# Feed-forward products of a decoder layer: 320 + 320 activation columns against the high weights, recut into two stretches of other widths

## The chip, the cores and the metric

The kernel runs on one NeuronCore of a Trainium2 chip. The metric is the device time of one execution in microseconds (us). Before the change it is 2118.0 us, the median of two runs (2117.37 and 2118.63). A measurement of this kernel tells a difference of about 2% from no change.

## What is computed

One decoder layer over 256 prompt tokens and 64 sample tokens, which the kernel carries side by side as 320 columns. The change touches its last part, the feed-forward block:

```python
hf = _rmsnorm(x, p['norm_ffn'])
x = x + (jax.nn.silu(hf @ p['w_ffn_gate']) * (hf @ p['w_ffn_up'])) @ p['w_ffn_down']
```

The width of `x` is 2048, the hidden width 5632, everything is float32. The rest (input projection, state-space branch, linear attention, memory attention, merge, output projection) is not touched.

## The kernel before, in words

Everything is stored transposed: features on the 128 partitions, the 320 tokens along the free dimension. A matrix product is done one block of 128 output features at a time. `load` brings the block's weights (1 MB, `raw`, three buffers) from memory, `parts` splits them into a high part `whi` (rounded to float32r, ScalarE, L79) and a low part `wlo = raw - whi` (VectorE, L80), two buffers each. The activations are split in the same way, here into `fh`/`fl` (input of the block) and `hidh`/`hidl` (hidden values). `mm3` (L91 to L93) sums three float32r products per 128 input features in one PSUM bank: high x high, high x low, low x high. Each of these matmuls is 128 x 128 weights by 320 columns and brings its own load of the weights.

The feed-forward block, `back`, runs in four quarters (`FQ`) of 11 hidden blocks (`FT`). Per hidden block there are a gate product and an up product, each over 16 chunks of 128 inputs (48 matmuls); their epilogues (L1202 to L1208 and `split`, L1073 and L1074) make one chunk of the hidden values. Then come 16 down products over the quarter's 11 hidden chunks (33 matmuls each), which are added to `x` (L1214). That makes 44 + 44 + 64 = 152 products with 12 x 176 = 2112 groups of three matmuls. In the last quarter `stats` sums squares for the final norm, whose `rstd` and scaling close the kernel. PSUM tiles come from `psum_mm`, which alternates between two pools (`pmm`, `psm`).

The order of the instructions on each engine is set by a scheduler when the kernel is built (`schedule_with_timeline_sim=True`). Engines run their instructions in that order and wait for each other through semaphores.

Of the kernel before, what the change touches and what calls it, by code (L numbers as in the profile page):

```python
# [8 lines left out]
F32 = mybir.dt.float32  # L9
F32R = mybir.dt.float32r  # L10
# [3 lines left out]
ALU = mybir.AluOpType  # L14
# [4 lines left out]
P = 128  # L19
D = 2048  # L20
KD = D // P
NP_, NS = 256, 64
NT = NP_ + NS
# [13 lines left out]
FT = FH // P // FQ  # L37
# [12 lines left out]
class Build:  # L50
# [36 lines left out]
    def mm3(self, ps, hi, lo, k0, nk, xh, xl, kx=0):  # L87
        nc = self.nc
        for k in range(nk):
            ws = slice((k0 + k) * P, (k0 + k + 1) * P)  # L90
            nc.tensor.matmul(ps, hi[:, ws], xh[:, kx + k, :], start=k == 0, stop=False)  # L91
            nc.tensor.matmul(ps, hi[:, ws], xl[:, kx + k, :], start=False, stop=False)  # L92
            nc.tensor.matmul(ps, lo[:, ws], xh[:, kx + k, :], start=False, stop=k == nk - 1)  # L93

    def together(self, products):

        first = products[0]().ins
        with self.tc.issue_after(first):
            for p in products[1:]:
                p()  # L100
# [975 lines left out]
    def back(self):  # L1076
        nc, io = self.nc, self.io
        TT = nc.vector.tensor_tensor
# [6 lines left out]
        for n, d in (("x", self.d_yx), ("g", self.d_yg)):  # L1085
            hi = yp.tile([P, 8, NT], F32R, name=f"y{n}h")
            lo = yp.tile([P, 8, NT], F32R, name=f"y{n}l")
# [15 lines left out]
        hi = yp.tile([P, 8, NT], F32R, name="ysh")  # L1103
        lo = yp.tile([P, 8, NT], F32R, name="ysl")
# [9 lines left out]
        for m2 in range(4):  # L1114
            wh, wl = self.unit(io["w_glu"][m2])
            for i in range(2):
                m = 2 * m2 + i
                ps = self.psum_mm()
# [38 lines left out]
        fp = self.push(self.left, "ffn", bufs=1)  # L1157
        x = fp.tile([P, KD, NT], F32, name="x")
        for c in range(4):
            nc.sync.dma_start(x[:, 4 * c : 4 * c + 4, :], io["xT"][:, 4 * c : 4 * c + 4, :])  # L1160
        fh = fp.tile([P, KD, NT], F32R, name="fh")
        fl = fp.tile([P, KD, NT], F32R, name="fl")
        ssum = fp.tile([P, NTP], F32, name="ssum")
        slast = fp.tile([P, NTP], F32, name="slast")
        for z in (ssum, slast):
# [3 lines left out]
        def stats(m):  # L1169
            sq = {0: ssum, KD - 1: slast}.get(m)  # L1170
            if sq is None:
                sq = fp.tile([P, NT], F32, name="sq", tag="sq", bufs=2)
            nc.scalar.square(sq[:, :NT], x[:, m, :])
            if m == KD - 1:
                return [ssum, slast]
            if m:
                TT(ssum[:, :NT], ssum[:, :NT], sq[:], op=ALU.add)

        for m in range(KD):
            wh, wl = self.unit(io["w_out"][m])  # L1180
            ps = self.psum_mm()
# [8 lines left out]
        nc.scalar.copy(rstd[:], self.rstd(sums, NT, 1.0 / D))  # L1190
        self.pop(self.right)
        dp = self.push(self.right, "hid", bufs=1)
        hh = dp.tile([P, FT, NT], F32R, name="hidh")
        hl = dp.tile([P, FT, NT], F32R, name="hidl")
        for q in range(FQ):
            for i in range(FT):
                m = q * FT + i
                wh, wl = self.unit(io["w_fg"][m])
                pg = self.psum_mm()
                self.mm3(pg[:, :NT], wh, wl, 0, KD, fh, fl)  # L1200
                s = dp.tile([P, NT], F32, name="fs", tag="fs", bufs=2)
                TT(s[:], pg[:, :NT], rstd[:], op=ALU.mult)  # L1202
                nc.scalar.activation(s[:], s[:], AF.Silu)
                TT(s[:], s[:], rstd[:], op=ALU.mult)
                wh, wl = self.unit(io["w_fu"][m])
                pu = self.psum_mm()
                self.mm3(pu[:, :NT], wh, wl, 0, KD, fh, fl)
                TT(s[:], pu[:, :NT], s[:], op=ALU.mult)  # L1208
                self.split(hh[:, i, :], hl[:, i, :], s[:])
            for m in range(KD):  # L1210
                wh, wl = self.unit(io["w_fd"][q, m], FT * P)
                ps = self.psum_mm()
                self.mm3(ps[:, :NT], wh, wl, 0, FT, hh, hl)
                TT(x[:, m, :], x[:, m, :], ps[:, :NT], op=ALU.add)  # L1214
                if q == FQ - 1:
                    sums = stats(m)
                    nc.scalar.mul(x[:, m, :], x[:, m, :], self.vec[:, C_FIN + m : C_FIN + m + 1])
# [120 lines left out]
```

## Time and profile before

| | |
|---|---|
| runs | 2117.37, 2118.63 us |
| profiled execution | 2118.14 us, of which the span of its instructions 2116.4 us |
| TensorE (PE) busy | 2088.3 us (99%), 14404 matmuls |
| VectorE (DVE) / ScalarE (ACT) busy | 1294.6 us (61%) / 848.8 us (40%) |
| DMA | 362.23 MB, mean 171 GB/s |

Times in the rows are in us from the first instruction, durations of single instructions in ns where a view says so. Matmuls overlap: a row of 0.31 us is a matmul from its start to its last result, while the next one starts earlier. So the cost of one in a stream is the distance between two starts. PE is the matmul stream, PEld the weight loads beside it.

### The profile page before, as it was taken

How to read it: one execution, taken by the hardware profiler on the slowest of the kernel's cores; microseconds unless marked ns; L12 is line 12 of the kernel's file. 1: busy time of each engine (PE TensorE's matmuls, PEld its weight loads, DVE VectorE, ACT ScalarE, POOL GpSimd, SP SyncE). 2: the span in 40 equal slices, each digit the busy share in tenths (PEclk: the TensorE clock that was granted, in tenths of full speed). 3: DMA queues.
4: the chain of work that ended last, by engine and by line, in shares of the span. 5: the costliest groups of instructions: out<-in, count | busy, mean ns of one | idle time of the engine just before them, and what ended most of it. 6: DMA issues, size and time to landing. Idle time of an engine off the chain costs nothing.

```text
span 2116.4 us, 34013 instructions
## 1 busy us (share of the span) xinstructions
PE 2088.3 (99%) x14404; PEld 2039.8 (96%) x14404; DVE 1294.6 (61%) x1964; ACT 848.8 (40%) x1117; POOL 161.3 (8%) x203
## 2 busy tenths in 40 slices
PE   9899999999999999999999999999999999999997
PEld 7899998999999999999999999999999999999997
DVE  7868779888997945675645444444444444444444
ACT  6445345554445344543434333233322333233343
POOL 8611011012101000000000000000000000000000
PEclk9999999999999999999999999999999999999998
DMA  9665665435454454765554443454434443454442
GB/s 342 216 221 207 216 215 182 149 132 184 140 178 149 149 191 156 263 208 192 199 182 152 140 158 125 148 167 159 140 129 170 160 140 129 151 179 142 145 137 105
DMA packets 72697, 362.23 MB, mean 171 GB/s; under 512 B 8032, under 2 KB 18144, under 8 KB 42720
## 3 DMA queue, kind: packets, MB, share of 16 engines
q1 hardware_dynamic: 72544, 360.05, 49.8%
q8 instruction: 113, 1.85, 0.4%
q14 instruction: 40, 0.33, 0.0%
HBM read 338.49 MB, written 21.53 MB: 170 GB/s over the span
## 4 chain that ended last, share of the span: by engine, by line
PE 91%; DVE 6%; ACT 1%; issue 1%; DMA 1%; SPq 0%; DVEq 0%; ACTq 0%
PE pmm L93 19%; PE pmm L91 19%; PE pmm L92 18%; PE psm L91 10%; PE psm L92 10%; PE psm L93 10%; DVE wlo L80 1%; DVE xr L355 0%; DVE s_w L626 0%; PE psm L903 0%; ACT whi L79 0%; PE psm L306 0%; PE psm L754 0%; PE bu L607 0%; PE psm L307 0%
## 5 line engine op out<-in xcount | busy, mean ns | idle before, releaser
L79 ACT CAST whi<-raw 128x2048 fp32r<-128x2048 f32 (+3 forms) x308 | 538.9, 1751 | 952.2 <-issue 536.8
L80 DVE TENSOR_TENSOR wlo<-raw,whi 128x2048 fp32r<-128x2048 f32 (+3 forms) x308 | 647.9, 2104 | 279.1 <-ACT whi L79 277.3
L93 PE MATMUL pmm<-hh,wlo 128*128 128x320 f32 x1408 | 438.6, 312 | 2.6 <-DVE wlo L80 2.6
L91 PE MATMUL pmm<-hh,whi 128*128 128x320 f32 x1408 | 439.2, 312 | 0.0
L92 PE MATMUL pmm<-hl,whi 128*128 128x320 f32 x1408 | 437.7, 311 | 0.0
L93 PEld LDWEIGHTS pmm<-hh,wlo 128*128 128x128 f32 x1408 | 264.4, 188 | 6.5 <-DVE wlo L80 3.1
L91 PEld LDWEIGHTS pmm<-hh,whi 128*128 128x128 f32 x1408 | 264.5, 188 | 5.8 <-issue 5.5
L92 PEld LDWEIGHTS pmm<-hl,whi 128*128 128x128 f32 x1408 | 264.5, 188 | 2.0 <-issue 1.3
L91 PE MATMUL psm<-fh,whi 128*128 128x320 f32 x704 | 217.6, 309 | 0.0
L91 PE MATMUL pmm<-fh,whi 128*128 128x320 f32 x704 | 217.6, 309 | 0.0
L92 PE MATMUL pmm<-fl,whi 128*128 128x320 f32 x704 | 217.6, 309 | 0.0
L92 PE MATMUL psm<-fl,whi 128*128 128x320 f32 x704 | 217.5, 309 | 0.0
L93 PE MATMUL psm<-fh,wlo 128*128 128x320 f32 x704 | 217.5, 309 | 0.0
L93 PE MATMUL pmm<-fh,wlo 128*128 128x320 f32 x704 | 217.5, 309 | 0.0
L91 PEld LDWEIGHTS psm<-fh,whi 128*128 128x128 f32 x704 | 132.1, 188 | 0.1
L92 PEld LDWEIGHTS pmm<-fl,whi 128*128 128x128 f32 x704 | 132.1, 188 | 0.0
L93 PEld LDWEIGHTS pmm<-fh,wlo 128*128 128x128 f32 x704 | 132.1, 188 | 0.0
L91 PEld LDWEIGHTS pmm<-fh,whi 128*128 128x128 f32 x704 | 132.1, 188 | 0.0
L92 PEld LDWEIGHTS psm<-fl,whi 128*128 128x128 f32 x704 | 132.1, 188 | 0.0
L93 PEld LDWEIGHTS psm<-fh,wlo 128*128 128x128 f32 x704 | 132.1, 188 | 0.0
L93 PE MATMUL pmm<-hidh,wlo 128*128 128x320 f32 x352 | 109.2, 310 | 0.0
L92 PE MATMUL pmm<-hidl,whi 128*128 128x320 f32 x352 | 108.8, 309 | 0.0
(431 smaller groups left out, 3687.1 us busy)
## 6 DMA issues: line engine op xcount, KB each, us to landing
raw<-w_in SPq DMA_DIRECT2D x88, 1024.0 KB, 4.9
raw<-w_fg SPq DMA_DIRECT2D x44, 1024.0 KB, 4.8
raw<-w_fu SPq DMA_DIRECT2D x44, 1024.0 KB, 4.9
raw<-w_fd SPq DMA_DIRECT2D x64, 704.0 KB, 4.1
raw<-w_br SPq DMA_DIRECT2D x24, 1024.0 KB, 4.9
at_kv<-kv SPq DMA_DIRECT2D x32, 512.0 KB, 6.3
raw<-w_out SPq DMA_DIRECT2D x16, 1024.0 KB, 4.9
raw<-w_mk SPq DMA_DIRECT2D x8, 1024.0 KB, 6.2
```

What stands on the lines that cost most here:

```text
L79: nc.scalar.copy(hi[:, s], raw[:, s])
L80: nc.vector.tensor_tensor(lo[:, s], raw[:, s], hi[:, s].bitcast(F32), op=ALU.subtract)
L91: nc.tensor.matmul(ps, hi[:, ws], xh[:, kx + k, :], start=k == 0, stop=False)
L92: nc.tensor.matmul(ps, hi[:, ws], xl[:, kx + k, :], start=False, stop=False)
L93: nc.tensor.matmul(ps, lo[:, ws], xh[:, kx + k, :], start=False, stop=k == nk - 1)
```

## The change

A new function `mm2` takes the place of `mm3` in the three products of the feed-forward block, and nowhere else. The high and the low part of the activations now lie side by side in one tile of 640 columns per chunk (`fx`, `hid`). The high weights meet these 640 columns in two matmuls of `cut` and `640 - cut` columns, which go to two PSUM banks `pa` and `pb`. The low weights meet the first 320 columns as before. So the three results are no longer summed in one bank: ScalarE copies the first 320 columns of `pa` into a tile `fsum`, and VectorE adds the rest of `pa` (if `cut` is over 320) and `pb` to it. `cut` differs by quarter and product:

| quarter | gate | up | down |
|---|---|---|---|
| 1 | 384 + 256 | 320 + 320 | 512 + 128 |
| 2 | 352 + 288 | 448 + 192 | 416 + 224 |
| 3 | 336 + 304 | 400 + 240 | 480 + 160 |
| 4 | 384 + 256 | 384 + 256 | 384 + 256 |

PSUM pairs now come in a cycle of three (`bu`, `pmm`, `psm`).

```diff
+    def mm2(self, hi, lo, nk, x, cut):
+        nc = self.nc
+        self.turn += 1
+        if self.turn % 3 == 0:
+            bu = self.pbu.tile([P, 2, 512], F32, name="bu", tag="bu", bufs=1)
+            pa, pb = bu[:, 0], bu[:, 1]
+        elif self.turn % 3 == 1:
+            pa, pb = (self.pmm.tile([P, 512], F32, name="pmm", tag="pmm", bufs=2)[:] for _ in range(2))
+        else:
+            pa, pb = (self.psum_sm()[:] for _ in range(2))
+        for k in range(nk):
+            ws = slice(k * P, (k + 1) * P)
+            nc.tensor.matmul(pa[:, :cut], hi[:, ws], x[:, k, :cut], start=k == 0, stop=False)
+            nc.tensor.matmul(pb[:, : 2 * NT - cut], hi[:, ws], x[:, k, cut:], start=k == 0, stop=k == nk - 1)
+            nc.tensor.matmul(pa[:, :NT], lo[:, ws], x[:, k, :NT], start=False, stop=k == nk - 1)
+        s = self.sums.tile([P, NT], F32, name="fsum", tag="fsum", bufs=2)
+        n = cut - NT
+        TT = nc.vector.tensor_tensor
+        nc.scalar.copy(s[:], pa[:, :NT])
+        if n:
+            TT(s[:, :n], s[:, :n], pa[:, NT:cut], op=ALU.add)
+        TT(s[:, n:], s[:, n:], pb[:, : 2 * NT - cut], op=ALU.add)
+        return s
...
-        fh = fp.tile([P, KD, NT], F32R, name="fh")
-        fl = fp.tile([P, KD, NT], F32R, name="fl")
+        fx = fp.tile([P, KD, 2 * NT], F32R, name="fx")
+        fh, fl = fx[:, :, :NT], fx[:, :, NT:]
...
-        hh = dp.tile([P, FT, NT], F32R, name="hidh")
-        hl = dp.tile([P, FT, NT], F32R, name="hidl")
+        hx = dp.tile([P, FT, 2 * NT], F32R, name="hid")
+        hh, hl = hx[:, :, :NT], hx[:, :, NT:]
+        self.sums = dp
+        cuts = ((384, 320, 512), (352, 448, 416), (336, 400, 480), (384, 384, 384))
...
-                pg = self.psum_mm()
-                self.mm3(pg[:, :NT], wh, wl, 0, KD, fh, fl)
+                pg = self.mm2(wh, wl, KD, fx, cuts[q][0])
...
-                pu = self.psum_mm()
-                self.mm3(pu[:, :NT], wh, wl, 0, KD, fh, fl)
+                pu = self.mm2(wh, wl, KD, fx, cuts[q][1])
...
-                ps = self.psum_mm()
-                self.mm3(ps[:, :NT], wh, wl, 0, FT, hh, hl)
+                ps = self.mm2(wh, wl, FT, hx, cuts[q][2])
```

Up to the first feed-forward product the order of the instructions is the same on every engine. In the block it differs at two kinds of places.

On VectorE, in the first quarter, one gate and one up epilogue with the weight splits between them stood so before:

```order
L1202 TENSOR_TENSOR fs_12548<-pmm_12499,rstd_11252 128x320
L80 TENSOR_TENSOR wlo_12613<-raw_12610,whi_12612 128x2048
L1204 TENSOR_TENSOR fs_12548<-fs_12548,rstd_11252 128x320
L1208 TENSOR_TENSOR fs_12548<-psm_12558,fs_12548 128x320
L80 TENSOR_TENSOR wlo_12672<-raw_12669,whi_12671 128x2048
L1074 TENSOR_TENSOR hidl_12258<-fs_12548,hidh_12257 128x320
```

Now the same stretch (`bu_12389` is the gate product, `pmm_12453` the up product) reads:

```order
L80 TENSOR_TENSOR wlo_12511<-raw_12508,whi_12510 128x2048
L117 TENSOR_TENSOR fsum_12438<-fsum_12438,bu_12389 128x64
L118 TENSOR_TENSOR fsum_12438<-fsum_12438,bu_12389 128x256
L1229 TENSOR_TENSOR fs_12442<-fsum_12438,rstd_11251 128x320
L1231 TENSOR_TENSOR fs_12442<-fs_12442,rstd_11251 128x320
L80 TENSOR_TENSOR wlo_12575<-raw_12572,whi_12574 128x2048
L118 TENSOR_TENSOR fsum_12502<-fsum_12502,pmm_12453 128x320
L1234 TENSOR_TENSOR fs_12442<-fsum_12502,fs_12442 128x320
L1100 TENSOR_TENSOR hid_12256<-fs_12442,hid_12256 128x320
```

The sums stand behind the weight split that becomes possible at the same product end, not ahead of it.

On TensorE, where the second quarter goes over from the up to the down products (`pmm_15495` is the first down product, `psm_15536` the second), the order before had, around the last chunk of the first one:

```order
L93 MATMUL pmm_15495<-hidh_12257,wlo_15492 128x320
L91 MATMUL psm_15536<-hidh_12257,whi_15532 128x320
L92 MATMUL psm_15536<-hidl_12258,whi_15532 128x320
L91 MATMUL pmm_15495<-hidh_12257,whi_15491 128x320
L93 MATMUL psm_15536<-hidh_12257,wlo_15533 128x320
L91 MATMUL psm_15536<-hidh_12257,whi_15532 128x320
```

Now, with the pairs `pmm_15762`/`pmm_15763` and `psm_15808`/`psm_15809` for these two products, the second one is nearly finished before the first one's last chunk. It begins with ten narrow matmuls in a row:

```order
L111 MATMUL pmm_15762<-hid_12256,wlo_15759 128x320
L109 MATMUL psm_15808<-hid_12256,whi_15804 128x416
L110 MATMUL psm_15809<-hid_12256,whi_15804 128x224 x10
L111 MATMUL psm_15808<-hid_12256,wlo_15805 128x320
```

It ends with the first one's last chunk and three more groups, ahead of the third down product (`bu_15854`):

```order
L109 MATMUL pmm_15762<-hid_12256,whi_15758 128x416
L110 MATMUL pmm_15763<-hid_12256,whi_15758 128x224
L111 MATMUL pmm_15762<-hid_12256,wlo_15759 128x320
L109 MATMUL psm_15808<-hid_12256,whi_15804 128x416
L111 MATMUL psm_15808<-hid_12256,wlo_15805 128x320
L109 MATMUL psm_15808<-hid_12256,whi_15804 128x416
L110 MATMUL psm_15809<-hid_12256,whi_15804 128x224
L111 MATMUL psm_15808<-hid_12256,wlo_15805 128x320
L109 MATMUL bu_15854<-hid_12256,whi_15850 128x416
```

So the number of matmuls left behind the last use of the first product's weights fell to five. The matmuls themselves are as many as before: three per group.

## Rows read from the trace of the kernel before

**Rows 1.** The page: busy time by engine, and the chain that ended last.
```profile
PE 2088.3 (99%) x14404; PEld 2039.8 (96%) x14404; DVE 1294.6 (61%) x1964; ACT 848.8 (40%) x1117; POOL 161.3 (8%) x203
PE 91%; DVE 6%; ACT 1%; issue 1%; DMA 1%; SPq 0%; DVEq 0%; ACTq 0%
```

**Rows 2.** Busy us by window (PE, PEld, DVE, ACT, POOL; then granted clock), second quarter.
```profile
1405.00:1560.00 155.00, 155.00 (x1059) 155.00 (x1058) 69.62 (x66) 48.84 (x44) 0.00 (x0) 1.00 0.43 145
1560.00:1637.00 77.00, 77.00 (x525) 76.80 (x524) 33.75 (x33) 22.91 (x16) 0.00 (x0) 1.00 0.47 159
```

**Rows 3.** Timeline of PE, a feed-forward product (start, duration, what): 320 columns.
```profile
1499.81 0.31 PE L91 MATMUL psm<-fh,whi 128*128 128x320 f32 x1
...
1501.87 0.31 PE L93 MATMUL pmm<-fh,wlo 128*128 128x320 f32 x1
```

**Rows 4.** Timeline of PE, memory values: float32r matmuls of 512 columns.
```profile
22.46 0.39 PE L307 MATMUL pmm<-whi,ml 128*128 128x512 f32 x1
...
25.20 0.39 PE L307 MATMUL pmm<-whi,ml 128*128 128x512 f32 x1
```

**Rows 5.** Timeline of PE, memory keys: float32r matmuls of 256 columns.
```profile
73.34 0.28 PE L91 MATMUL pmm<-mh,whi 128*128 128x256 f32 x1
...
78.75 0.28 PE L92 MATMUL pmm<-ml,whi 128*128 128x256 f32 x1
```

**Rows 6.** Timeline of PE, plain float32 matmuls of 128 and 64 columns.
```profile
422.57 0.38 PE L547 MATMUL psm<-ident,s_bd 128*128 128x128 f32 x2
...
423.01 0.56 PE L903 MATMUL psm<-gl_qk 128*128 128x64 f32 x4
...
423.61 0.31 PE L92 MATMUL pmm<-hl,whi 128*128 128x320 f32 x1
```

**Rows 7.** Timeline at the end: weight loads of six one-column matmuls.
```profile
2101.41 0.74 PEld L126 LDWEIGHTS psm<-ones,slast 128*128 128x128 f32 x6 [0.60 <-ACT slast L1173]
```

**Rows 8.** Timeline of PE: one plain float32 matmul of 256 columns, then float32r.
```profile
136.90 0.60 PE L720 MATMUL psm<-kT,at_q 128*128 128x256 f32 x2
137.14 0.49 PE L91 MATMUL pmm<-hh,whi 128*128 128x320 f32 x1
137.47 0.31 PE L92 MATMUL pmm<-hl,whi 128*128 128x320 f32 x1
```

**Rows 9.** Timelines of DVE and ACT at a product end in the gate and up stage.
```profile
1501.23 1.91 ACT L79 CAST whi<-raw 128x2048 fp32r<-128x2048 f32 x1 [4.76 <-issue]
...
1503.04 0.45 ACT L1073 CAST hidh<-fs 128x320 fp32r<-128x320 f32 x1
...
1503.17 2.29 DVE L80 TENSOR_TENSOR wlo<-raw,whi 128x2048 fp32r<-128x2048 f32 x1 [1.34 <-ACT whi L79]
```

**Rows 10.** Timelines of DVE and ACT at a product end in the down stage.
```profile
1368.74 1.38 ACT L79 CAST whi<-raw 128x1408 fp32r<-128x1408 f32 x1 [3.46 <-PE pmm L92]
...
1370.15 1.62 DVE L80 TENSOR_TENSOR wlo<-raw,whi 128x1408 fp32r<-128x1408 f32 x1 [0.78 <-ACT whi L79]
...
1373.73 0.49 DVE L1214 TENSOR_TENSOR x<-x,psm 128x320 f32<-128x320 f32 x1 [1.95 <-PE psm L93]
```

**Rows 11.** Timeline of DVE, first quarter, from the up to the down products.
```profile
1325.13 0.49 DVE L1208 TENSOR_TENSOR fs<-psm,fs 128x320 f32<-128x320 f32 x1 [3.71 <-PE psm L93]
...
1327.98 0.48 DVE L1074 TENSOR_TENSOR hidl<-fs,hidh 128x320 fp32r<-128x320 f32 x1
...
1333.33 1.63 DVE L80 TENSOR_TENSOR wlo<-raw,whi 128x1408 fp32r<-128x1408 f32 x1 [0.81 <-ACT whi L79]
1334.87 0.48 DVE L1214 TENSOR_TENSOR x<-x,psm 128x320 f32<-128x320 f32 x1
```

**Rows 12.** Timeline at the end: last product, its sum, a short VectorE operation.
```profile
2100.02 0.31 PE L93 MATMUL psm<-hidh,wlo 128*128 128x320 f32 x1
...
2100.36 0.49 DVE L1214 TENSOR_TENSOR x<-x,psm 128x320 f32<-128x320 f32 x1 [3.32 <-PE psm L93]
...
2102.27 0.16 DVE L134 TENSOR_SCALAR rs_v<-psm 128x3 f32<-128x3 f32 x1 [1.42 <-PE psm L126]
```

## The prediction

> **What bounds the kernel now.** I read the page first. PE is busy 99% of the span, and the chain that ended last is PE for 91% of it [rows 1]. Then the windows of the feed-forward block: in the second quarter PE is busy for 155.00 of 155.00 us and 77.00 of 77.00 us, at a granted clock of 1.00 (2.4 GHz), while DVE is busy for 45% and ACT for 32% [rows 2]. The other quarters read the same. So nothing waits there but on PE, and what a change is worth is read from the distance between the starts of matmuls. In a feed-forward product that distance is (1501.87 - 1499.81) / 14 = 0.147 us for 320 columns [rows 3]; a product of 48 matmuls takes 7.04 us, one of 33 takes 4.84 us, and the 2112 groups of three take 2112 x 0.440 = 929 us of the 2116.4.
>
> **What a width costs.** The change leaves the number of matmuls, of weight loads and of columns as it is: 320 + 320 + 320 per group becomes cut + (640 - cut) + 320. It can only pay or cost by how the price depends on the width. The trace has two more widths in float32r: 512 columns take (25.20 - 22.46) / 12 = 0.2283 us [rows 4], 256 columns take (78.75 - 73.34) / 46 = 0.1176 us [rows 5]. From 320 to 512 a column costs 0.425 ns, from 256 to 320 it costs 0.455 ns; both lines keep some 10 to 13 ns per matmul. Between these widths I interpolate.
>
> No float32r matmul narrower than 256 is in the trace, and the change makes five such widths: 128, 160, 192, 224 and 240. They are the unknown cost. Each brings its own load of 128 x 128 weights, for which a narrow stream leaves little cover. The nearest rows are the plain float32 ones, which are recorded as two matmuls with a load each. From 422.57 to 423.61 there are eight of them, 128 or 64 columns wide (two on L547, a transpose; two on L897 at 422.78; four on L903), and one of 320 [rows 6]: (1.04 - 0.147) / 8 = 0.112 us each, and the 64-column ones are no cheaper than the 128-column ones. Six loads for one-column matmuls take 0.74 us [rows 7], at most 0.12 us apart. So a pair of load and matmul seems to have a floor of about 0.11 us whatever the width, and the 256-column row at 0.1176 us lies just over it. I take **0.115 us** for all five narrow widths, between 0.112 and 0.1176, because both neighbours are that near. The lower end is the slope of the 256-to-320 line carried on (0.059 us at 128 columns, 0.110 at 240). The upper end is the price of plain float32, far off: one such matmul of 256 columns takes from 136.90 to 137.47 less one 320-column matmul, 0.423 us or 1.65 ns a column [rows 8].
>
> The two high-weight matmuls of a group cost 2 x 146.7 = 293.4 ns now. After the change, in ns:
>
> 384 + 256: 173.9 + 117.6 = 291.5, so -1.9, in four stages. 320 + 320: 0. 512 + 128: 228.3 + 115 = 343.3, +49.9. 352 + 288: 160.3 + 132.2, -0.9. 448 + 192: 201.1 + 115, +22.7. 416 + 224: 187.5 + 115, +9.1. 336 + 304: -0.5. 400 + 240: 180.7 + 115, +2.3. 480 + 160: 214.7 + 115, +36.3.
>
> The sum over the twelve stages is 111 ns, and each has 176 groups: **+19.6 us**. With a floor of 0.1176 it is 21.9 us.
>
> The Trainium skill, page "TensorE: Matmul & The Clock Gate", section "LDWEIGHTS (loading the stationary operand)", gives a load of 128 columns as columns / 1.2 ns, an estimate of 107 ns. The rows show loads only beside matmuls, at 0.112 us or more; by that floor the term would be 13.1 us instead of 19.6.
>
> **The new epilogue.** Per product it adds one ACT copy of 320 columns (0.45 us, as the 320-column cast [rows 9]) and one or two DVE sums over 320 columns together. A 320-column DVE operation takes 0.49 us and a 3-column one 0.16 us [rows 12], so a pair costs about 0.65 us. What is queued behind them are the weight splits for later products. A product's end frees the weight buffers; then come the cast (1.91 us) and the subtraction (2.29 us) of the product after next [rows 9]. In the new order the subtraction stands ahead of the sums, so the weights are ready 4.2 us after a product's end, as before, against a period of 7.04 us. The `raw` buffers come free at the same point, so the loads on SP's queue don't move. Behind it the gate epilogue (sums, multiply, Silu on ACT, multiply) ends at 4.2 + 0.65 + 0.49 + 0.45 + 0.49 = 6.3 us, ahead of the next cast. In the down stage cast and subtraction take 1.38 + 1.62 us [rows 10], the sums and the addition to x end at 3.05 + 0.65 + 0.49 = 4.2 us of 4.84. In the last quarter one more DVE addition for the norm (0.49 us) brings that to 4.7. So I cost this at nothing inside a stage; if the subtraction stood behind the sums it would be ready at 6.7 of 7.04 us, still in time. PSUM does not bind: a pair comes back after three products.
>
> It is not free at two places. At the turn from up to down products the last hidden chunk comes later: before, its low part was done at 1328.46, 3.3 us after the up epilogue began at 1325.13 [rows 11]; with the subtraction (to 1328.05), sums, multiply, ACT's cast and the low part in a row it is about 5.0 us. The order puts more of the second down product ahead of the first one's last chunk, so less is left behind it to hide the cast and subtraction for the third. Before, that subtraction ended at 1334.96, when the sum of the finished second product had already begun (1334.87) [rows 11]: there is no spare. In the second quarter six matmuls are left behind the last use of the high weights (0.93 us, of which 0.16 is the matmul's own way to its end). The cast needs 1.43 us, so PE waits 0.66 us; then the subtraction's 1.63 us has two matmuls (0.30 us) over it, so 1.35 us more. The same reckoning gives 0, 0.3 and 0.7 us in the first, third and fourth quarter, where more is left or a run of high-weight matmuls opens the third product: **+3.0 us**. The bounds are 0, if the waits overlap with what PE still has, and 4 x 2.0 = 8 us.
>
> At the end of the block the last sum has nothing over it: 0.45 + 0.65 us come ahead of the addition to x, **+1.1 us**. What leads to the block and the final norm is unchanged.
>
> **The sum** against the profiled execution: 2118.14 + 19.6 + 3.0 + 1.1 = 2141.8 us, +1.1%. That execution lies within 0.2 us of the median 2118.0, so the forecast for the median is 2142.
>
> **Rivals.** *No floor, the price stays a line.* Each row that was read at 256 columns or more is on a line, and narrow float32 rows may owe their 0.112 us to their two passes. Then the five widths cost 59 to 110 ns, 140 ns less per twelve groups: 19.6 - 24.6 = -5.0 us, and with the two epilogue terms at 0 to 4.1 the time is 2113 to 2117, likeliest 2117: not slower. It decides from a floor under 0.067 us. Against it stand rows 6 and 7, where 64 columns cost as much as 128 and one column nearly as much. The same page's section "Back-to-back issue gap" gives a lone matmul as columns / 2.4 + 2.5 ns, which would be this case; 320 columns would be 136 ns by it, and the trace has 147.
>
> *Narrow float32r falls to the price of plain float32.* Nothing in the trace shows the fast rate below 256 columns. At 1.65 ns a column the five cost 211, 264, 317, 370 and 396 ns, 983 ns more than at the floor: 983 x 176 = 173 us on top, 2315 us. At half that price per column (the cost of one of its two passes) they cost 115, 132, 158, 185 and 198 ns, 213 ns more: 37 us on top, 2179 us. For it: the only narrow matmuls in the trace are the slow kind. Against it: the rate at 256 columns is already so near the floor of rows 6 and 7 that a load explains everything, and a step from 118 ns at 256 to 396 ns at 240 columns would be odd. It decides where a narrow column costs over about 0.75 ns.
>
> *The epilogue becomes the bound.* If sums and copy took 1 us longer than I cost them, the down products would run on the chain cast, subtraction, sums, addition instead of PE: 5.7 us against 4.84 in quarter four, 5.2 against 4.94 in quarter two (its 224-column floor counted), so 16 x 0.86 + 16 x 0.26 = 18 us, 2160. Against it: DVE is busy for under half of these windows [rows 2].
>
> **How the numbers follow.** Floor near 0.115 us, 2134 to 2147: 0.65. Line without floor, 2113 to 2121: 0.09. Half the float32 price, 2179: 0.05. Full float32 price, 2315: 0.17. Epilogue, 2160: 0.03. A gain I can't name: 0.01. The range from 2113 to 2180 holds 0.83 of it. About 2% (42 us) is what a measurement tells from no change: faster 0.01, within 2% 0.77, slower 0.22.
>
> **What would show it.** After: matmuls of 128, 160 and 192 columns that start about 0.115 us before the next one, whatever their width; the gate, up and down windows of quarter four as long as before; the down stage of quarter one longer by 8.8 us (176 x 49.9 ns), that of quarter three by 6.4. PE waits on ACT and DVE only at the turns, 3 us in all. I am wrong if the 240- and 224-column stages are the slowest: then the price follows the columns at another rate. I am wrong the other way if the 128-column matmuls take 60 ns.

## The result and the profile after

The changed kernel takes 2144.81 us, the median of two runs (2144.06 and 2145.55), against 2118.0 before: 1.0127 times as long, 95% interval 1.0083 to 1.017. The forecast was 2142. Slower, by less than the 2% that count as a difference.

The page of the changed kernel, busy time by engine and the chain that ended last, answers to [rows 1].

```profile
PE 2113.9 (99%) x14404; PEld 2048.8 (96%) x14404; DVE 1371.6 (64%) x2257; ACT 904.9 (42%) x1269; POOL 158.3 (7%) x203
PE 90%; DVE 7%; ACT 1%; DMA 1%; issue 1%; SPq 0%; DVEq 0%; ACTq 0%
```

The matmuls are as many as before, 14404, and PE still ends the kernel, but it is busy for 25.6 us more. DVE gained 77 us and ACT 56 us of work. Where that lies is seen in the windows of the second quarter (gate and up, then down), which answer to [rows 2].

```profile
1414.00:1571.00 157.00, 157.00 (x1052) 154.76 (x1051) 81.07 (x109) 58.07 (x65) 0.00 (x0) 1.00 0.43 146
1572.00:1653.00 81.00, 79.33 (x526) 77.87 (x525) 41.53 (x64) 27.73 (x33) 0.00 (x0) 1.00 0.43 146
```

DVE is at half of the window, and PE waits for nothing in the gate and up stage. In the down stage it is busy for 79.33 of 81.00 us; the rest is the turn from up to down products, below.

The cost of a width is read from the starts on PE. This is the timeline of the first quarter's down stage (512 + 128), which answers to [rows 3 to 5], and below it the weight loads of the same stretch (PEld).

```profile
1336.70 0.39 PE L109 MATMUL bu<-hid,whi 128*128 128x512 f32 x1
1336.93 0.22 PE L110 MATMUL bu<-hid,whi 128*128 128x128 f32 x1
1336.99 0.36 PE L111 MATMUL bu<-hid,wlo 128*128 128x320 f32 x1
1337.19 0.39 PE L109 MATMUL bu<-hid,whi 128*128 128x512 f32 x1
```
```profile
1336.93 0.19 PEld L111 LDWEIGHTS bu<-hid,wlo 128*128 128x128 f32 x1
1337.04 0.19 PEld L109 LDWEIGHTS bu<-hid,whi 128*128 128x128 f32 x1
1337.19 0.19 PEld L110 LDWEIGHTS bu<-hid,whi 128*128 128x128 f32 x1
```

From 512 to 128 columns it is 0.23 us, from 128 to 320 only 0.06, and from 320 to the next 512 it is 0.20, where 320 columns alone cost 0.147. So a group takes 0.49 us instead of 0.44. The matmul of 128 columns looks cheap, and the one behind it pays. The loads say why. The load for the 320-column matmul starts at 1336.93, when the 128-column matmul starts, and the next load comes at 1337.04, 0.11 us later: the 320 columns can't run before their weights are in. One load hides behind the matmul ahead of it, and 128 columns don't last as long as it.

The other narrow widths do the same. These are rows of the up stage of quarter two (448 + 192) and of quarter three (400 + 240).

```profile
1440.42 0.25 PE L110 MATMUL bu<-fx,whi 128*128 128x192 f32 x1
1440.50 0.33 PE L111 MATMUL bu<-fx,wlo 128*128 128x320 f32 x1
1440.67 0.36 PE L109 MATMUL bu<-fx,whi 128*128 128x448 f32 x1
```
```profile
1759.90 0.27 PE L110 MATMUL psm<-fx,whi 128*128 128x240 f32 x1
1760.01 0.31 PE L111 MATMUL psm<-fx,wlo 128*128 128x320 f32 x1
1760.16 0.34 PE L109 MATMUL psm<-fx,whi 128*128 128x400 f32 x1
```

At 192 columns the pair takes 0.08 + 0.17 = 0.25 us, 0.10 more than the 320 columns alone; at 240 it is 0.11 + 0.15. Over the rows where a 320-column matmul stands behind the narrow one, the medians of the two distances together, less 147 ns, are 113 ns (128 columns), 112 (160), 110 (192), 110 (224), 113 (240) and 116 (256): one price up to 240.

From the starts of the first matmul of each stage (timeline of PE) I made this table, in us. "Before" is the length, the others are the difference to it.

| stage | before | changed | e1_all320 | e2_widths | e7_third |
|---|---|---|---|---|---|
| 1 gate, up (384, 320) | 157.56 | 0.04 | 0.01 | 0.04 | -0.33 |
| 1 down (512) | 77.64 | 8.69 | 0.39 | 8.57 | 8.00 |
| 2 gate, up (352, 448) | 154.88 | 3.00 | 0.00 | 3.00 | 3.01 |
| 2 down (416) | 77.65 | 4.00 | 1.36 | 1.82 | 2.09 |
| 3 gate, up (336, 400) | 154.88 | 0.46 | 0.00 | 0.46 | 0.59 |
| 3 down (480) | 77.65 | 6.62 | 0.38 | 6.13 | 6.24 |
| 4 gate, up (384, 384) | 154.88 | 0.03 | 0.00 | 0.03 | 0.00 |
| 4 down (384) | 77.51 | 0.77 | 0.39 | -0.10 | -0.20 |
| whole block | 932.65 | 23.61 | 2.53 | 19.94 | 19.40 |

(The first stage holds the norm's 2.7 us. In e1 every cut is 320.)

The turn into the second quarter's down products, timelines of PE, ACT and DVE around the third one, answers to [rows 11].

```profile
1580.53 0.27 PE L110 MATMUL pmm<-hid,whi 128*128 128x224 f32 x1
...
1582.29 0.46 PE L109 MATMUL bu<-hid,whi 128*128 128x416 f32 x1 [0.57 <-ACT whi L79]
1582.59 0.26 PE L110 MATMUL bu<-hid,whi 128*128 128x224 f32 x1
1583.95 0.42 PE L111 MATMUL bu<-hid,wlo 128*128 128x320 f32 x1 [1.10 <-DVE wlo L80]
```
```profile
1580.87 1.37 ACT L79 CAST whi<-raw 128x1408 fp32r<-128x1408 f32 x1 [4.61 <-PE pmm L110]
```
```profile
1582.27 1.63 DVE L80 TENSOR_TENSOR wlo<-raw,whi 128x1408 fp32r<-128x1408 f32 x1 [5.49 <-ACT whi L79]
```

The last use of the first product's high weights starts at 1580.53. Then come the cast, the first matmul of the third product, the subtraction and its first low-weight matmul in a chain, and PE waits for 0.57 and 1.10 us. All waits of PE in the block are in the list of its waits from 1169 us on (line waited for, us in total, times, longest).

```profile
PE psm L152 <- ACT slast L1199: 1.6, 1, 1.6
PE bu L111 <- DVE wlo L80: 1.1, 1, 1.1
PE bu L109 <- ACT whi L79: 0.6, 1, 0.6
PE pmm L109 <- ACT whi L79: 0.5, 1, 0.5
```

Three of them are at turns, 2.2 us in all: two in the second quarter (0.57 and 1.10 us) and one in the fourth (0.5 us, at 2058.17). The other one is at the end, where the timeline answers to [rows 12].

```profile
2126.12 0.31 PE L111 MATMUL psm<-hid,wlo 128*128 128x320 f32 x1
...
2126.47 0.42 ACT L115 COPY fsum<-psm 128x320 f32<-128x320 f32 x1 [2.22 <-PE psm L111]
2126.93 0.22 DVE L117 TENSOR_TENSOR fsum<-fsum,psm 128x64 f32<-128x64 f32 x1 [2.74 <-ACT fsum L115]
2127.07 0.41 DVE L118 TENSOR_TENSOR fsum<-fsum,psm 128x256 f32<-128x256 f32 x1
2127.51 0.49 DVE L1239 TENSOR_TENSOR x<-x,fsum 128x320 f32<-128x320 f32 x1
```

The addition to x starts 1.39 us after the start of the last matmul, before the change 0.34 us after it: 1.05 us more. The spans from that start to the end (the tail) are 16.35 us before and 17.64 us now, so the tail cost 1.3 us. The block began 2.5 us later in this execution (first matmul at 1169.86 against 1167.37) although its instructions up to there stand in the same order. Three windows show most of why (granted clock third from the end).

```profile
0.00:60.00 60.00, 56.95 (x265) 47.28 (x266) 45.34 (x86) 39.09 (x49) 53.73 (x122) 0.97 0.86 317
60.00:120.00 60.00, 55.06 (x429) 54.26 (x428) 50.89 (x71) 26.97 (x40) 25.64 (x33) 0.94 0.68 242
380.00:400.00 20.00, 17.44 (x109) 17.18 (x108) 18.42 (x35) 8.69 (x13) 0.00 (x0) 0.91 0.42 144
```

The mean granted clock is 0.97, 0.94 and 0.91 here, in the same windows before the change 1.00, 0.97 and 1.00; parts of these stretches ran at 1.2 instead of 2.4 GHz. By the starts on PE the same matmuls come about 1.3 us late at 94 us and about 1.5 us more after 387 us; a few tenths of that are gone again before the block. In the run with 512 + 128 everywhere the first two windows read 0.94 and 0.94, and its block begins at 1174.94; with the widths but without the epilogue (e2 below) it begins at 1166.69. This moves from execution to execution and not with the change. So block and tail are compared by their own lengths: 23.6 + 1.3 = 24.9 us.

### The profile page after: what moved, and what is told of

It reads as the page before. It is cut to its first block, busy times and chain, and to the rows that moved or that the text cites. A ratio compares the mean times of both kernels' runs of the same rounds, so it can differ in the third digit from the quotient of the medians.

```text
span 2143.8 us, 34680 instructions
## 1 busy us (share of the span) xinstructions
PE 2113.9 (99%) x14404; PEld 2048.8 (96%) x14404; DVE 1371.6 (64%) x2257; ACT 904.9 (42%) x1269; POOL 158.3 (7%) x203
## 4 chain that ended last, share of the span: by engine, by line
PE 90%; DVE 7%; ACT 1%; DMA 1%; issue 1%; SPq 0%; DVEq 0%; ACTq 0%
PE pmm L91 11%; PE pmm L93 11%; PE pmm L92 11%; PE pmm L109 6%; PE psm L109 6%; PE bu L109 6%; PE bu L111 5%; PE psm L111 5%; PE pmm L111 5%; PE pmm L110 4%; PE psm L110 4%; PE bu L110 4%; PE psm L91 2%; PE psm L93 2%; PE psm L92 2%; DVE wlo L80 2%
## 5 line engine op out<-in xcount | busy, mean ns | idle before, releaser
L109 PE MATMUL pmm<-fx,whi 128*128 128x384 f32 (+5 forms) x480 | 159.7, 333 | 0.0
L109 PE MATMUL bu<-fx,whi 128*128 128x384 f32 (+5 forms) x464 | 155.0, 334 | 0.0
L109 PE MATMUL psm<-fx,whi 128*128 128x384 f32 (+5 forms) x464 | 153.7, 332 | 0.0
L111 PE MATMUL pmm<-fx,wlo 128*128 128x320 f32 x480 | 150.4, 313 | 0.0
L111 PE MATMUL bu<-fx,wlo 128*128 128x320 f32 x464 | 145.3, 313 | 0.0
L111 PE MATMUL psm<-fx,wlo 128*128 128x320 f32 x464 | 144.8, 312 | 0.0
L110 PE MATMUL pmm<-fx,whi 128*128 128x256 f32 (+5 forms) x480 | 134.0, 283 | 0.0
L110 PE MATMUL bu<-fx,whi 128*128 128x256 f32 (+5 forms) x464 | 130.7, 282 | 0.0
L110 PE MATMUL psm<-fx,whi 128*128 128x256 f32 (+5 forms) x464 | 129.6, 284 | 0.0
L109 PEld LDWEIGHTS pmm<-fx,whi 128*128 128x128 f32 x480 | 90.5, 188 | 0.0
L110 PEld LDWEIGHTS pmm<-fx,whi 128*128 128x128 f32 x480 | 89.4, 188 | 0.0
```

Source lines behind the costliest of these rows:

```text
L109: nc.tensor.matmul(pa[:, :cut], hi[:, ws], x[:, k, :cut], start=k == 0, stop=False)
L110: nc.tensor.matmul(pb[:, : 2 * NT - cut], hi[:, ws], x[:, k, cut:], start=k == 0, stop=k == nk - 1)
L111: nc.tensor.matmul(pa[:, :NT], lo[:, ws], x[:, k, :NT], start=False, stop=k == nk - 1)
```

## Experiments

The theory: a load of 128 x 128 weights takes about 0.11 us, one load is hidden behind the matmul ahead, so a matmul narrower than that costs as much as the load; the new epilogue is hidden inside the stages and costs only at turns and tail. The rivals: the epilogue, or the two banks, cost the time; or narrow columns cost more each. The runs are called e1 to e8 below, as in the table. Of e3, e4, e5, e6 and e8 there is one execution each, so they are read by the length of the block.

**The epilogue without narrow matmuls (e1).**

```diff
-        cuts = ((384, 320, 512), (352, 448, 416), (336, 400, 480), (384, 384, 384))
+        cuts = ((320, 320, 320),) * 4
```

> The changed kernel with cut 320 in all twelve stages: two banks, copy and sums on reading as in the change, but no matmul narrower than 320. Theory (a load and a matmul together take at least 0.111 us, so only widths under about 230 cost): the stage lengths fall back to those before within 0.3 us except for the turns and the tail, together 3 to 4 us, so 2121 to 2122 us. Rival (the new epilogue or the two banks cost the time): nothing comes back, 2142 to 2145 us.

Measured: 2123.28 us beside 2121.96 of the kernel before on the same chip, ratio 1.0013 (1.0002 to 1.0023). In the table the gate and up stages are back to 0.01 us, the four down stages keep 2.5 us of turns, and the tail is 17.50 us, +1.15. The time in microseconds lies over the expected one, and in this set the kernel before was 4 us slower too. The ratio, of the means, is +2.7 us (0.4 to 4.9), and block and tail are +3.7 us, where 3 to 4 were expected. Copy, sums and banks cost nothing inside a stage.

**The widths without the epilogue (e2).** The matmuls are those of the changed kernel; the copy and the sums are gone, and the epilogue reads the first 320 columns of `pa` alone.

```diff
-        s = self.sums.tile([P, NT], F32, name="fsum", tag="fsum", bufs=2)
...
-        return s
+        return pa
```

> The changed kernel's matmuls with all its widths, but the product is read straight from the first 320 columns of the first bank, as before the change: no copy, no sums. It leaves out the high x low part of every feed-forward product. Theory: the width term alone, +19 to +20 us, 2137 to 2139 us (the turns back to nothing or nearly so). Rival (epilogue): within 3 us of 2118.

Measured: 2140.19 us, 1 us over the expected range, beside the same 2121.96; ratio 1.0091 (1.0074 to 1.0108), and the block is 19.94 us longer. In the stages where a narrow width stands the table has nearly the same numbers as in the changed kernel: 8.57 for 8.69, 3.00 for 3.00, 6.13 for 6.62. So most of the time is in the widths. Together with e1 it gives 19.94 + 2.53 = 22.5 of the block's 23.6 us; the missing 1.1 us is mostly where both meet, at the turns (second quarter: 1.82 + 1.36 against 4.00).

**512 + 128 everywhere (e3).**

```diff
-        cuts = ((384, 320, 512), (352, 448, 416), (336, 400, 480), (384, 384, 384))
+        cuts = ((512, 512, 512),) * 4
```

> The changed kernel with 512 + 128 in all twelve stages. Theory: every group pays what the first quarter's down stage paid, 8.69 us / 176 = 49 ns, so 2112 x 49 = 104 us and 3 to 4 us for turns and tail: 2224 to 2228 us. Rival (the stage of 128 columns was long because of its epilogue or the run of eleven narrow matmuls at its start, at its place in the program): the other eleven stages pay less than 20 ns a group, under 2170 us.

Measured: 2232.02 us. The block is 1037.6 us long, +105.0, 49.7 ns for each of the 2112 groups. So it is not the place of that stage in the program. The time is 4 us over the expected; the block began 7.6 us late in this execution, most of it at the lower clock (above).

**Another order in the group (e6).** 512, 320, 128 instead of 512, 128, 320.

```diff
             nc.tensor.matmul(pa[:, :cut], hi[:, ws], x[:, k, :cut], start=k == 0, stop=False)
+            nc.tensor.matmul(pa[:, :NT], lo[:, ws], x[:, k, :NT], start=False, stop=k == nk - 1)
             nc.tensor.matmul(pb[:, : 2 * NT - cut], hi[:, ws], x[:, k, cut:], start=k == 0, stop=k == nk - 1)
-            nc.tensor.matmul(pa[:, :NT], lo[:, ws], x[:, k, :NT], start=False, stop=k == nk - 1)
```

> 512 + 128 in all stages as before in e3, but in each group the low-weight matmul (320) stands between the two high-weight ones, so that the order is 512, 320, 128. Theory (one load at a time can be hidden behind the matmul ahead of it, so each matmul takes the longer of its columns and 0.111 us): no change, 2229 to 2234 us. Rival (a long matmul can hide more than one load ahead, so neighbours matter): the order moves the time by over 20 us.

Measured: 2227.78 us, 1 us under the expected range, block 1040.9 us, 3.3 us more than in the other order; they lie in the gate and up stages of the last three quarters, 1.1 to 1.2 us in each, and their cause is not shown. The timeline of PE shows that the wait has moved to the 512-column matmul, which now stands behind the narrow one.

```profile
1500.24 0.22 PE L111 MATMUL bu<-fx,whi 128*128 128x128 f32 x1
1500.30 0.45 PE L109 MATMUL bu<-fx,whi 128*128 128x512 f32 x1
1500.58 0.31 PE L110 MATMUL bu<-fx,wlo 128*128 128x320 f32 x1
1500.73 0.22 PE L111 MATMUL bu<-fx,whi 128*128 128x128 f32 x1
```

0.06 us behind the narrow one, then 0.28 instead of 0.23 us for the 512 columns: the same 0.05 us, paid by whoever comes next. The 320 columns ahead hide one load, and not the next one too.

**The floor by itself (e4).** The kernel before, with a fourth matmul in each feed-forward group, 32 columns wide, into a spare bank.

```diff
...
             nc.tensor.matmul(ps, lo[:, ws], xh[:, kx + k, :], start=False, stop=k == nk - 1)
+            if extra:
+                wx = slice((k0 + k) * P, (k0 + k) * P + 128)
+                nc.tensor.matmul(junk[:128, 0, :32], hi[:, wx], xh[:, kx + k, :32], start=True, stop=True)
...
```

> The kernel before with a fourth matmul in each of the 2112 groups: the same high weights once more, against 32 columns, into a spare bank that nobody reads. Theory (floor of load and matmul, whatever the width): 0.111 us each, +234 us, 2350 to 2355 us. Rival (cost follows the columns, some 0.013 us + 0.42 ns a column): 0.027 us each, +56 us, 2174 us. Rival (narrow columns dearer, 1.65 ns each as plain float32): 0.053 us or what the line adds, 2230 us at most.

Measured: 2353.10 us; the block is 1165.0 us, +232.4, 0.110 us for each of 2112. Neither rival comes near. 32 columns cost what 128 and 192 do.

**Fewer weight columns in it (e5 and e8).** `wx` and `junk` cut to 64 and to 32 weight columns.

> As the run with an extra 32-column matmul per group, but the extra one takes only 64 of the 128 weight columns. Theory A (the floor is the time to load the weights, a column at a time): half the floor, 0.055 us each, +117 us, 2235 to 2240 us. Theory B (a fixed time of any load and matmul pair): 0.111 us each as before, 2353 us.

> The same with 32 weight columns. Theory A: a quarter of the floor or what the 32 columns themselves cost, 0.027 to 0.03 us each, +56 to +65 us, 2175 to 2185 us. Theory B: 2353 us. Theory C (loads are made in full blocks of columns, whatever is asked): the same as with 64 or with 128.

Measured: 2315.44 and 2287.28 us, the block +193.0 and +168.2 us. That is 0.091 and 0.080 us each: neither expectation, and my theory had missed something. The scheduler put these matmuls in two kinds of places in all three kernels: 1212 stand alone between wide ones, 900 in 151 runs, nearly all of six. First the rows of PE with 64, then with 32, then those with 128 weight columns.

```profile
1405.69 0.47 PE L98 MATMUL bu<-hidh,whi 128*64 128x32 f32 x6
1407.48 0.18 PE L98 MATMUL bu<-hidh,whi 128*64 128x32 f32 x1
1408.04 0.18 PE L98 MATMUL bu<-hidh,whi 128*64 128x32 f32 x1
```
```profile
1408.93 0.34 PE L98 MATMUL bu<-hidh,whi 128*32 128x32 f32 x6
1410.04 0.18 PE L98 MATMUL bu<-hidh,whi 128*32 128x32 f32 x1
1410.59 0.18 PE L98 MATMUL bu<-hidh,whi 128*32 128x32 f32 x1
```
```profile
1405.87 0.74 PE L98 MATMUL bu<-hidh,whi 128*128 128x32 f32 x6
1407.93 0.18 PE L98 MATMUL bu<-hidh,whi 128*128 128x32 f32 x1
1408.48 0.18 PE L98 MATMUL bu<-hidh,whi 128*128 128x32 f32 x1
```

A row "x6" lasts from the start of the first to the end of the last, so in the runs of six the distance is (0.74 - 0.18) / 5 = 0.112 us with 128 weight columns, (0.47 - 0.18) / 5 = 0.058 with 64 and (0.34 - 0.18) / 5 = 0.032 with 32: the load's time goes by the weight columns. But where the matmul stands alone a group takes 0.55 us in all three kernels, 0.11 more than the 0.44 of three matmuls, whatever the narrow one's own weights are. It is the load of the matmul **behind** it that isn't hidden, and that one has 128 columns. The loads beside the second of these 64-column rows show it.

```profile
1407.34 0.13 PEld L98 LDWEIGHTS bu<-hidh,whi 128*64 128x64 f32 x1
1407.49 0.19 PEld L93 LDWEIGHTS psm<-hidh,whi 128*128 128x128 f32 x1
1407.60 0.19 PEld L94 LDWEIGHTS psm<-hidl,whi 128*128 128x128 f32 x1
```

The narrow one's own load starts at 1407.34, under the 320 columns ahead of it. The load for the matmul behind it starts at 1407.49, with the narrow one, and the next load comes 0.11 us later. The last of a run, too, has 128 weight columns behind it. So 1212 + 151 = 1363 of these matmuls have a load of 128 columns behind them and 749 one of their own kind: with 64 columns 1363 x 0.110 + 749 x 0.058 = 193 us, as measured; with 32 it is 174 against 168, and the last 6 us are not explained.

The Trainium skill, page "TensorE: Matmul & The Clock Gate", section "LDWEIGHTS (loading the stationary operand)", gives weight columns / 1.2 ns, by estimate 107, 53 and 27 ns. The runs show 112, 58 and 32 ns, some 5 ns more each.

**A third pair of weight buffers (e7)**, for the turns.

```diff
+        self.n_unit += 1
+        if self.sums is not None and self.n_unit % 3 == 0:
+            hi = self.sums.tile([P, 2048], F32R, name="whi", tag="whi3", bufs=1)
+            lo = self.sums.tile([P, 2048], F32R, name="wlo", tag="wlo3", bufs=1)
+        else:
...
```

> The changed kernel with a third pair of buffers for the weight parts in the feed-forward block. Theory (at the turns from up to down products PE waits for the cast and the subtraction of the third down product, because its buffer comes free only with the first product's late last chunk): the four down stages lose these waits, second quarter from 4.0 to about 1.7 us over before, the others by 0.4 to 0.9 us, together 3 to 4 us, 2141 us. Rival (the turns cost by something else: the late hidden chunk itself, PSUM): stage lengths as in the changed kernel within 0.5 us, 2145 us.

Measured: 2142.27 us beside 2119.07 before, ratio 1.0105 (1.0088 to 1.0123), which overlaps the changed kernel's own interval. The stage lengths tell more: the second down stage falls from 4.00 to 2.09 us over before, the others by 0.4 to 1.0 us, the block by 4.2 us. PE's waits on casts and subtractions are gone from its list, which over the same window is

```profile
PE psm L186 <- DVE rs_out L178: 2.3, 1, 2.3
PE psm L158 <- ACT slast L1205: 1.6, 1, 1.6
```

with both waits behind the last product (the final norm's `rs_out` was waited for 2.2 us before the change too). So the waits at the turns are those on the weight buffers.

None of these edits makes a kernel that is faster than the one before.

## Why the prediction was right, and where it was not

*What bounds the kernel, and that only the width matters.* Right: PE is at 157.00 of 157.00 us in the second gate and up stage, as it was, and e2 alone has 19.94 us in the block.

*The width term, +19.6 us.* Right in sum (19.9 by e2), and near stage by stage: 8.8 forecast and 8.57 measured for 512 + 128, 6.4 and 6.13 for 480 + 160, 1.6 and 1.82 for 416 + 224, 3.8 and 3.00 for 352 and 448. The floor is a little lower than the 0.115 us taken, 0.110 to 0.113 us. Against that, some wide partners are a little dearer than interpolated (0.232 us at 512 where 0.2283 was read), and the stages of 384 + 256, forecast as 1.3 us of gain together, gained nothing (0.04, 0.03 and -0.10 us in e2). That these nearly cancel is luck: the sum is nearer than its parts.

*The mechanism of the floor.* Half right. It is the weight load, and it doesn't depend on the width. But the prediction let a matmul pay for its own load. The load that isn't hidden is that of the next matmul (e5_w64, e8_w32). With equal weights everywhere, as in this change, both give the same sum, so the sum came out right although the payer was wrong. It also named the wrong sign to look for: starts 0.115 us behind each narrow matmul. They are 0.06 us behind the 128 columns, and the prediction had said it would be wrong if they were. The 0.05 us stand with the matmul after.

*The epilogue at nothing.* Right (e1: gate and up stages within 0.01 us).

*The turns, +3.0 us.* Right in kind and about in size. PE waits 2.2 us there; the second quarter's two waits were forecast as 0.66 and 1.35 us and are 0.57 and 1.10, the fourth quarter's as 0.7 and is 0.5, and the third quarter's 0.3 is not in the list. By the table the epilogue costs the block 23.61 - 19.94 = 3.7 us over e2, and with the third buffers the block gets 4.2 us shorter.

*The tail, +1.1 us:* 1.3 us.

*The rivals.* The line without a floor (2113 to 2117) falls with e4: 32 columns would have cost 0.027 us there, and cost 0.110. The price of plain float32 (2315), or half of it (2179), falls with the medians above: 240 columns would have cost 0.396 or 0.198 us, and cost 0.113, no more than 128. (e4 alone doesn't decide this one, as 32 columns at that price stay under the floor.) The epilogue as the bound falls with e1.

The sum agrees to 3 us. In the profiled execution block and tail are 24.9 us longer where 23.7 were forecast, and 2.5 us are in the part before the block, where the clock differed.

## What to carry to other kernels

In the dense streams here each matmul costs the longer of its own columns and the weight load of the one behind it: with 128 weight columns in float32r, 32 columns and 128 to 240 columns all cost 0.110 to 0.113 us, and 256 cost 0.116. So when columns are split over matmuls the split should leave each piece at about 240 columns or more. A narrow piece was cheaper only where the matmul behind it had few weight columns (32 columns: 0.058 us with 64, 0.032 with 32). A start-to-start distance behind one matmul isn't its price; add up a whole group.

## What the runs showed that I had not expected

Five to eleven narrow matmuls that the scheduler gathered cost as much as single ones (0.111 us each at 128, 160 and 224 columns, by the start of the first and of the second matmul behind the run), so with equal weights their places hardly matter for the sum. And a lone 32-column matmul with 32 weight columns, 0.032 us by itself in a run, costs 0.11 us between wide ones, more than three times as much.
